# Scan products by 64-row halves in turn, and a rotation of score banks, in a two-network kernel on one core

## The chip, the core and the metric

The kernel runs on one core of a Trainium2 chip. The core has TensorE for matrix products (it writes into PSUM, eight banks of 128 partitions by 512 fp32 columns), VectorE, ScalarE and GpSimd for everything element by element, SyncE which mainly issues transfers, and 16 DMA engines. Each engine works through its own list of instructions in order; semaphores tie the lists together. The metric is device time of one execution in microseconds; less is better. [...]

## The reference, cut to what matters

Two small networks run one after the other on 256 tokens of width 1024. The first layer of the first network has two mixers side by side for 256 latent and 256 context tokens: a gated delta rule that is scanned in chunks of 64 tokens, in both directions, and a latent attention with eight heads. The scan of one direction, cut:

```
def step(s, inp):
    u_i, w_i, qk_i, qd_i, kd_i, gl_i = inp
    v_new = u_i - einsum('bhck,bhkv->bhcv', w_i, s)
    o_i = einsum('bhck,bhkv->bhcv', qd_i, s) + einsum('bhcs,bhsv->bhcv', qk_i, v_new)
    s = s * gl_i[..., None, None] + einsum('bhck,bhcv->bhkv', kd_i, v_new)
    return s, o_i
```

There are 8 heads, keys and values of 64, and 512 tokens (context first, then latent), so 8 steps in each direction, 16 in all. The attention, cut:

```
s = einsum('bqkgd,bskd->bkgqs', q_i, k).astype(float32) * scale
p = softmax(s, axis=-1)
return einsum('bkgqs,bskd->bqkgd', p, v)
```

Context tokens see 256 keys, latent tokens 512.

## The kernel before

All is in fp32. Large products split each operand into a high and a low part (`whi`, `wlo`) and are three products (`mm3`, L554 to L556); ScalarE casts the high part (L270), VectorE or GpSimd subtracts for the low part (L272). Weights come by SyncE's queue into a ring of raw buffers (`wraw`), two in this stretch. Small fp32 products are given to TensorE as they are; each of them is two instructions there.

A scheduler with its own model of time sets the order in which each engine's instructions stand; a tile (PSUM bank or buffer) is handed on in the order in which the program asks for tiles of its kind. In the first layer PSUM has kinds `g` (three banks, also what `aux` asks for), `s` (two, also `acc`), `tp`, `po` and `gv` (one each).

The scan is `gdn_run`. Its outer loop has four blocks of 128 tokens (two chunks, one in partitions 0 to 63, the other in 64 to 127); inside it come the two directions `d`. `gdn_operands` (L1142) makes, for a direction and block, `u` (L1158), `w` transposed (L1160) and the queries transposed (L1163) in three `g` banks, which ScalarE copies to `gu` and `gwq` (L1165 to L1169), and loads `Q` (the masked query-key products) by SyncE's queue (L1171). `gdn_state` then does one step: operands times state (L1192), the difference `gvn` on VectorE (L1195), the state products (L1199, four of 128 columns, of which the 64x64 blocks on the diagonal are used), the decay of the state on GpSimd (L1206), its sum on VectorE (L1207), and the query products (L1210, eight of 64 columns); `gdn_o` adds results to the output (L1177). `gdn_post` follows (L1238 to L1245).

After the scan in the program, and mixed with it by the scheduler, come six modulation products (`mod_chunk`: loads L370, products L373, columns L386) and `l0_mla`. It works by four pairs of heads; a pair's queries and keys are projected (L849 to L857), then four query tiles go through `attend`: scores, maximum (L676), exponential (L678), transposes into the same bank (L681), copy `pt` (L683), row sums (L699), value products (L689). Score banks are both `s` in pairs 0 and 1, one `s` and one `g` in pairs 2 and 3, whose projections use `g` as well. The buffers `p` and `pt` are two each (`K.np`).

Of the kernel before, what the change touches and what calls it, by code (L numbers as in the profile page):

```python
# [15 lines left out]
ALU = mybir.AluOpType  # L16
# [192 lines left out]
def aux(K):  # L209
    return bank(K, "aux")  # L210
# [576 lines left out]
def l0_mla(K, O):  # L787
# [44 lines left out]
    for t in range(4):  # L832
# [2 lines left out]
        mm3(K, ps, ch[:, tk], cl[:, tk], wkh[:, 1, :], wkl[:, 1, :], True, True)  # L835
        nc.scalar.copy(vt[:, t, :], ps)
    wq = None
    for pair in range(4):
        heads = {}
        for h in (2 * pair, 2 * pair + 1):  # L840
            if h % 4 == 0:
                wq = WQ.load(K.ins["w_q"], 0, 2, (h // 4) * 512, 512)
            late = "g" if pair >= 2 else None
            ps = bank(K, late or "acc")
            hs = slice((h % 4) * 128, (h % 4 + 1) * 128)
            for k in range(2):
                mm3(K, ps, wq[0][:, k, hs], wq[1][:, k, hs], qh[:, k, :], ql[:, k, :], k == 0, k == 1)
            u = cut(K, [128, 512], F32, "p", K.np)
            nc.vector.tensor_tensor(u, ps, K.c("qtab"), op=ALU.mult)  # L849
            q1, q2 = cut(K, [128, 512], FR, "q1", 2), cut(K, [128, 512], FR, "q2", 2)  # L850
            split(K, q1, q2, u)
            ps = bank(K, late or "acc")
            hs = slice(h * 64, (h + 1) * 64)
            mm3(K, ps[:64, :], wkh[:, 0, hs], wkl[:, 0, hs], ch, cl, True, True)
            k1, k2 = kh[h % 2], kl[h % 2]
            nc.scalar.copy(k1[:64, :], ps[:64, :])
            nc.vector.tensor_tensor(k2[:64, :], ps[:64, :], k1.bitcast(F32)[:64, :], op=ALU.subtract)  # L857
            heads[h] = (q1, q2, k1, k2)
        po, rb = bank(K, "po"), bank(K, "gv")
        for t in range(4):  # L860
            n = 256 if t < 2 else 512

            def score(pss):
                tk = slice(t * 128, (t + 1) * 128)
                for hh in range(2):
                    q1, q2, k1, k2 = heads[2 * pair + hh]
                    mm3(K, pss[hh][:, :n], q1[:, tk], q2[:, tk], k1[:, :n], k2[:, :n], True, True)
                    yield pss[hh][:, :n]
            attend(K, score, lambda hh, j: vt[:, j, pair * 128 + hh * 64:pair * 128 + hh * 64 + 64], po, rb, t * 128,
                   ("s", "g") if late else ("s", "s"))  # L870
        nc.scalar.copy(O[:, pair, :], rb)
        nc.vector.tensor_tensor(O[:, pair, :], po, O[:, pair, :], op=ALU.mult)

# [264 lines left out]
def gdn_operands(K, d, t):  # L1140

    nc = K.nc  # L1142
    q, k, v = K.qkv
    P = K.P[d]
    tv = lambda x: x[:, t, :].rearrange("p (h d) -> p h d", h=8)
    sc = lambda x: bc(x[:, t * 8:(t + 1) * 8], [128, 8, 64], 2)
    ke = cut(K, [128, 8, 64], F32, "gke", 1)
    qe = cut(K, [128, 512], F32, "gqe", 1).rearrange("p (h d) -> p h d", h=8)
    kd = cut(K, [128, 512], F32, "gkd", 2)
    nc.vector.tensor_tensor(ke, tv(k), sc(K.eg[d]), op=ALU.mult)  # L1150
    nc.vector.tensor_tensor(qe, tv(q), sc(K.eg[d]), op=ALU.mult)
    nc.gpsimd.tensor_tensor(kd.rearrange("p (h d) -> p h d", h=8), tv(k), sc(K.ekd[d]), op=ALU.mult)
    pu, pw = aux(K), [aux(K), aux(K)]
    for h in range(8):
        hs = slice(h * 64, h * 64 + 64)
        for a in range(2):
            r = slice(a * 64, a * 64 + 64)
            nc.tensor.matmul(pu[r, hs], P[r, t, h, :], v[r, t, hs], start=True, stop=True)  # L1158
            o = (h // 2) * 64
            nc.tensor.matmul(pw[a][(h % 2) * 64:(h % 2) * 64 + 64, o:o + 64], ke[r, h, :], P[r, t, h, :],  # L1160
                             start=True, stop=True)
    for p in range(4):
        nc.tensor.transpose(pw[p // 2][:, 256 + p % 2 * 128:384 + p % 2 * 128], qe[:, 2 * p:2 * p + 2, :].rearrange("p h d -> p (h d)"), K.ident)  # L1163
    u = cut(K, [128, 512], F32, "gu", 2)
    nc.scalar.copy(u, pu)  # L1165
    wq = cut(K, [128, 4, 4, 64], F32, "gwq", 2)
    for a in range(2):
        nc.scalar.copy(wq[:, :, 3 * a, :], pw[a][:, :256].rearrange("p (q c) -> p q c", q=4))
        nc.scalar.copy(wq[:, 2 * a:2 * a + 2, 1:3, :], pw[a][:, 256:].rearrange("p (q a c) -> p q a c", q=2, a=2))  # L1169
    Q = cut(K, [128, 8, 64], F32, "gQ", 2)  # L1170
    nc.sync.dma_start(Q, K.Qd[d, t].rearrange("p (h c) -> p h c", h=8))  # L1171
    return u, wq, kd, Q


def gdn_o(K, t, a, o, ps):
    if (t, a) in K.owritten:
        K.nc.vector.tensor_tensor(K.O[o, t, :], K.O[o, t, :], ps[o], op=ALU.add)  # L1177
    else:
        K.owritten.add((t, a))
        K.nc.scalar.copy(K.O[o, t, :], ps[o])  # L1180


def gdn_state(K, d, first, t, a, u, wq, kd, Q, S):
    nc = K.nc
    r = slice(64 * a, 64 * a + 64)
    o = slice(64 - 64 * a, 128 - 64 * a)
    if first:
        vn = u
    else:
        ps = aux(K)  # L1190
        for p in range(4):
            nc.tensor.matmul(ps[:, p * 128:(p + 1) * 128], wq[:, p, 2 * a:2 * a + 2, :].rearrange("p x c -> p (x c)"),  # L1192
                             S[:, p, :], start=True, stop=True)
        vn = cut(K, [128, 512], F32, "gvn", 2)
        nc.vector.tensor_tensor(vn[r], u[r], ps[r], op=ALU.subtract)  # L1195
    pS, po = aux(K), aux(K)
    for p in range(4):
        c = slice(p * 128, (p + 1) * 128)
        nc.tensor.matmul(pS[:, c], kd[r, c], vn[r, c], start=True, stop=True)  # L1199
    pSv = pS.rearrange("p (q c) -> p q c", q=4)  # L1200
    for hh in range(2):
        x = slice(hh * 64, hh * 64 + 64)
        if first:
            nc.vector.tensor_copy(S[x, :, x], pSv[x, :, x])
        else:
            nc.gpsimd.tensor_tensor(S[x, :, x], S[x, :, x], bc(K.glc[d][x, t, a, :], [64, 4, 64], 2), op=ALU.mult)  # L1206
            nc.vector.tensor_tensor(S[x, :, x], S[x, :, x], pSv[x, :, x], op=ALU.add)  # L1207
    for h in range(8):
        hs = slice(h * 64, h * 64 + 64)
        nc.tensor.matmul(po[o, hs], Q[r, h, :], vn[r, hs], start=True, stop=True)  # L1210
    if not first:
        gdn_o(K, t, a, o, ps)
    gdn_o(K, t, a, o, po)


def gdn_run(K):
    K.owritten = set()
    for i in range(4):
        for d in range(2):
            t = i if d == 0 else (1, 0, 3, 2)[i]  # L1220
            ops = gdn_operands(K, d, t)
            for a in ((0, 1) if d == 0 else (1, 0)):
                gdn_state(K, d, i == 0 and a == d, t, a, *ops, K.S[d])


def gdn_post(K):
# [951 lines left out]
```

## Time and profile before

| | |
|---|---|
| median of 3 runs | 2125.01 us (2121.82 to 2138.47) |
| the profiled execution | 2124.6 us |
| its span, first to last instruction | 2122.8 us |
| mean granted clock | 0.957 |
| TensorE busy | 1991.6 us, 94% |
| VectorE busy | 1315.5 us, 62% |
| ScalarE busy | 924.7 us, 44% |
| scan and latent attention | about 269 to 456 us of the span |

Busy time of an engine is the union of its instructions' durations. [...] Idle time is put down to what released the engine. A stretch in which an engine is busy all the time at a low clock is longer than its work.

### The profile page before, as it was taken

The numbers are of one execution on the slowest core, as the hardware profiler recorded it, in microseconds if no ns is written. First come the engines' busy times: TensorE is split into PE (matmuls) and PEld (weight loads), VectorE is DVE, ScalarE is ACT, GpSimd is POOL, SyncE is SP. The second block draws the span as 40 slices with busy tenths as digits, with TensorE's granted clock in tenths as the row PEclk, the third lists the DMA queues.
The fourth block names the chain that finished last, engine by engine and source line by source line (L and its number), as shares of the span: only waits on it lengthen the run. The fifth ranks groups of instructions, "written<-read, shape, count | busy, mean of one in ns | idle before, by whom it ended". The sixth has DMA issues, their size and how long they took to land.

```text
span 2122.8 us, 31144 instructions
## 1 busy us (share of the span) xinstructions
PE 1991.6 (94%) x11656; PEld 1626.7 (77%) x11656; DVE 1315.5 (62%) x2729; ACT 924.7 (44%) x1620; POOL 242.1 (11%) x312
## 2 busy tenths in 40 slices
PE   6989799889999999979898999998999999989998
PEld 3868468768888778868666888897788789868886
DVE  5557457766777754454786555575765558576644
ACT  4533443354222233343565443564554445555532
POOL 2120212301000000020401001110200021020000
PEclk8999789899999999989898999998999999999999
DMA  8344542132568542213235664522656535055551
GB/s 284 90 120 101 179 130 66 46 109 80 179 213 279 164 158 90 89 53 120 70 99 159 184 194 137 155 87 62 197 179 190 180 97 147 21 169 184 188 188 66
DMA packets 186951, 291.88 MB, mean 137 GB/s; under 512 B 28472, under 2 KB 75704, under 8 KB 186800
## 3 DMA queue, kind: packets, MB, share of 16 engines
q1 hardware_dynamic: 172720, 272.54, 41.2%
q0 software_dynamic: 5472, 16.13, 2.4%
q10 hardware_dynamic: 8608, 1.23, 0.5%
q8 instruction: 91, 1.49, 0.3%
q14 instruction: 60, 0.49, 0.1%
HBM read 281.44 MB, written 8.41 MB: 137 GB/s over the span
## 4 chain that ended last, share of the span: by engine, by line
PE 85%; DVE 5%; DMA 4%; ACT 3%; issue 2%; POOL 1%; SPq 0%; ACTq 0%; DVEq 0%; POOLq 0%
PE acc L554 19%; PE acc L556 19%; PE acc L555 19%; PE s L554 3%; PE s L555 2%; PE s L556 2%; PE po L689 2%; PE tp L890 2%; PE po L1540 1%; PE tp L1540 1%; DMA wraw<-in_w_mod_dram 1%; PE gv L373 1%; PE aux L728 1%; PE aux L489 1%; PE g L1199 1%
## 5 line engine op out<-in xcount | busy, mean ns | idle before, releaser
L272 DVE TENSOR_TENSOR wlo<-wraw,whi 128x512 fp32r<-128x512 f32 (+4 forms) x772 | 483.4, 670 | 299.1 <-ACT whi L270 283.3
L270 ACT CAST whi<-wraw 128x1024 fp32r<-128x1024 f32 (+4 forms) x420 | 413.5, 990 | 496.4 <-PE acc L556 192.9
L554 PE MATMUL acc<-whi,u 128*128 128x512 f32 (+3 forms) x1320 | 508.5, 388 | 15.4 <-ACT u L306 9.6
L556 PE MATMUL acc<-whi,u 128*128 128x512 f32 (+3 forms) x1320 | 505.2, 384 | 1.7 <-DVE u L307 1.7
L555 PE MATMUL acc<-wlo,u 128*128 128x512 f32 (+3 forms) x1320 | 506.0, 385 | 0.2 <-DVE wlo L272 0.2
L554 PEld LDWEIGHTS acc<-whi,u 128*128 128x128 f32 x1320 | 251.3, 191 | 66.0 <-ACT u L306 11.6
L556 PEld LDWEIGHTS acc<-whi,u 128*128 128x128 f32 x1320 | 251.0, 190 | 50.4 <-DVE u L307 3.8
L555 PEld LDWEIGHTS acc<-wlo,u 128*128 128x128 f32 x1320 | 251.4, 191 | 47.4 <-DVE wlo L272 1.4
L554 PE MATMUL acc<-u,whi 128*128 128x512 f32 (+1 forms) x480 | 171.0, 362 | 1.8 <-ACT u L306 1.7
L555 PE MATMUL acc<-u,whi 128*128 128x512 f32 (+1 forms) x480 | 171.0, 358 | 0.2 <-DVE u L307 0.2
L556 PE MATMUL acc<-u,wlo 128*128 128x512 f32 (+1 forms) x480 | 171.1, 360 | 0.0
L272 POOL TENSOR_TENSOR wlo<-wraw,whi 128x512 fp32r<-128x512 f32 (+1 forms) x68 | 84.7, 1276 | 409.7 <-ACT whi L270 409.7
L432 DVE SCALAR_TENSOR_TENSOR msum<-mraw,u,msum 128x512 f32<-128x512 f32 x140 | 100.8, 747 | 15.2 <-DMA mraw<-in_w_mod_dram 14.1
L554 PEld LDWEIGHTS acc<-u,whi 128*128 128x128 f32 x480 | 91.0, 191 | 17.4 <-issue 2.6
L555 PEld LDWEIGHTS acc<-u,whi 128*128 128x128 f32 x480 | 91.9, 192 | 15.0 <-issue 1.7
L556 PEld LDWEIGHTS acc<-u,wlo 128*128 128x128 f32 x480 | 91.5, 191 | 15.0 <-issue 1.7
L307 DVE TENSOR_TENSOR u<-aux,u 128x512 fp32r<-128x512 f32 (+2 forms) x96 | 59.5, 632 | 41.0 <-ACT u L306 40.8
L554 PE MATMUL acc<-whi,dxh 128*128 128x512 f32 x176 | 69.7, 396 | 1.9 <-ACT dxh L306 1.9
L306 ACT CAST u<-aux 128x512 fp32r<-128x512 f32 (+2 forms) x96 | 50.6, 543 | 47.6 <-PE aux L728 34.9
L555 PE MATMUL acc<-wlo,dxh 128*128 128x512 f32 x176 | 69.6, 396 | 0.0
L556 PE MATMUL acc<-whi,dxl 128*128 128x512 f32 x176 | 69.0, 396 | 0.0
L307 DVE TENSOR_TENSOR dxl<-u,dxh 128x1024 fp32r<-128x1024 f32 x22 | 26.7, 1225 | 52.5 <-ACT dxh L306 52.5
(521 smaller groups left out, 3089.6 us busy)
## 6 DMA issues: line engine op xcount, KB each, us to landing
wraw<-in_w_up_dram SPq DMA_DIRECT2D x64, 512.0 KB, 4.0
wraw<-in_w_down_dram SPq DMA_DIRECT2D x64, 512.0 KB, 4.0
mraw<-in_w_mod_dram SPq DMA_DIRECT2D x56, 512.0 KB, 4.7
wraw<-in_w_ffn_down_dram SPq DMA_DIRECT2D x44, 512.0 KB, 3.8
wraw<-in_w_mod_dram SPq DMA_DIRECT2D x40, 512.0 KB, 5.9
wraw<-in_w_ffn_gate_dram SPq DMA_DIRECT2D x48, 256.0 KB, 3.1
wraw<-in_w_ffn_up_dram SPq DMA_DIRECT2D x48, 256.0 KB, 3.6
wraw<-in_w_ffn_gate_dram SPq DMA_DIRECT2D x20, 512.0 KB, 4.5
```

Source lines behind the costliest of these rows:

```text
L270: self.K.nc.scalar.copy(hi, raw)
L272: e.tensor_tensor(lo[:, k], raw[:, k], hi.bitcast(F32)[:, k], op=ALU.subtract)
L306: (hi_eng or nc.scalar.copy)(hi, src)
L307: nc.vector.tensor_tensor(lo, src, hi.bitcast(F32), op=ALU.subtract)
L373: nc.tensor.matmul(ps[32 * j:32 * j + 32, :], K.cl[:, g + k, :], raw[:, k, :], start=(g + k < 4), stop=(g + k >= 4))
L432: nc.vector.scalar_tensor_tensor(accs[s], raw[:, k, :], c, accs[s], op0=ALU.mult, op1=ALU.add)
L554: mm(ps, ah, bh, start=start, stop=False)
L555: mm(ps, ah, bl, start=False, stop=False)
L556: mm(ps, al, bh, start=False, stop=stop)
L689: nc.tensor.matmul(po[hh * 64:hh * 64 + 64, c:c + 128], v(hh, j), pts[hh][0][:, j * 128:(j + 1) * 128], start=(j == 0), stop=(j == nj - 1))
L890: nc.tensor.matmul(tp[:, t * 128:(t + 1) * 128], x[:, t // 2, t % 2 * 128 + j:t % 2 * 128 + j + 128], dg[j], start=(j == 0), stop=(j == 4))
L1540: nc.tensor.matmul(ps[t][:, c * 128:c * 128 + 128], yp[:, c, t * 128 + j:t * 128 + j + 128] if j < 31 else ones, dg, start=(j == 0), stop= ...
```

## The change

In the scan the two directions of a block are taken together: operands of both first, then for each of the two halves a step of either direction, which stand in opposite halves of the partitions. The state products become eight of 64x64 and 64 columns instead of four of 128 columns: only the diagonal blocks, by the column halves in turn. The query products of the two directions go into one bank, a head of one direction and the same head of the other in turn, so that the row and the column half switch at each product. The addition of the product with the state (`gdn_o` of `ps`) stands before the state products in the program.

In the latent attention `p` and `pt` get three buffers, and the score banks rotate: `s`, `s`, `tp` in pairs 0 and 1, `s`, `s`, `tp`, `g`, `g`, `g` in pairs 2 and 3.

```diff
@@ l0_mla
+    used = [0]
+    def unit(kinds):
+        used[0] += 2
+        return [kinds[(used[0] + i) % len(kinds)] for i in range(2)]
+    K.np = 3
     for pair in range(4):
...
             attend(K, score, lambda hh, j: vt[:, j, pair * 128 + hh * 64:pair * 128 + hh * 64 + 64], po, rb, t * 128,
-                   ("s", "g") if late else ("s", "s"))
+                   unit(("s", "s", "tp", "g", "g", "g") if late else ("s", "s", "tp")))
...
+    K.np = 2
@@ gdn_state
-def gdn_state(K, d, first, t, a, u, wq, kd, Q, S):
+def gdn_state(K, d, first, t, a, u, wq, kd, S):
...
         nc.vector.tensor_tensor(vn[r], u[r], ps[r], op=ALU.subtract)
-    pS, po = aux(K), aux(K)
+        gdn_o(K, t, a, slice(64 - 64 * a, 128 - 64 * a), ps)
+    pS = aux(K)[:, :256].rearrange("p (q c) -> p q c", q=4)
     for p in range(4):
-        c = slice(p * 128, (p + 1) * 128)
-        nc.tensor.matmul(pS[:, c], kd[r, c], vn[r, c], start=True, stop=True)
-    pSv = pS.rearrange("p (q c) -> p q c", q=4)
+        for hh in range(2):
+            c = slice(p * 128 + hh * 64, p * 128 + hh * 64 + 64)
+            nc.tensor.matmul(pS[hh * 64:hh * 64 + 64, p, :], kd[r, c], vn[r, c], start=True, stop=True)
...
-            nc.vector.tensor_tensor(S[x, :, x], S[x, :, x], pSv[x, :, x], op=ALU.add)
-    for h in range(8):
-        hs = slice(h * 64, h * 64 + 64)
-        nc.tensor.matmul(po[o, hs], Q[r, h, :], vn[r, hs], start=True, stop=True)
-    if not first:
-        gdn_o(K, t, a, o, ps)
-    gdn_o(K, t, a, o, po)
+            nc.vector.tensor_tensor(S[x, :, x], S[x, :, x], pS[x], op=ALU.add)
+    return vn
@@ gdn_run
-        for d in range(2):
-            t = i if d == 0 else (1, 0, 3, 2)[i]
-            ops = gdn_operands(K, d, t)
-            for a in ((0, 1) if d == 0 else (1, 0)):
-                gdn_state(K, d, i == 0 and a == d, t, a, *ops, K.S[d])
+        ts = [i, (1, 0, 3, 2)[i]]
+        ops = [gdn_operands(K, d, ts[d]) for d in range(2)]
+        for s in range(2):
+            vns = []
+            for d in range(2):
+                u, wq, kd, Q = ops[d]
+                a = s ^ d
+                vns.append((64 * a, Q, gdn_state(K, d, i == 0 and s == 0, ts[d], a, u, wq, kd, K.S[d])))
+            po = aux(K)
+            for h in range(8):
+                hs = slice(h * 64, h * 64 + 64)
+                for a, Q, vn in vns:
+                    K.nc.tensor.matmul(po[64 - a:128 - a, hs], Q[a:a + 64, h, :], vn[a:a + 64, hs], start=True, stop=True)
+            for d in range(2):
+                a = s ^ d
+                gdn_o(K, ts[d], a, slice(64 - 64 * a, 128 - 64 * a), po)
```

The scheduler draws new orders for all engines from this. Three places follow; a row is the line in that kernel's own file, the operation, the tile written and those read. In the changed kernel L1166, L1168 and L1171 are the operand products, L1200 operands times state, L1209 the state products, L1237 the query products, L1173 the copy of `gu`.

On TensorE, the end of the scan before, from the last direction's last transposes on (`g_3964` is a projection of pair 2):

```order
L1163 MATMUL g_3051<-const_id_75,gqe_3044 128x128 x2
L1192 MATMUL g_3097<-u_130,gwq_3090 128x128 x4
L1199 MATMUL g_3104<-gvn_3102,gkd_3045 128x128 x4
L1210 MATMUL g_3105<-gvn_3102,gQ_3095 64x64 x8
L1192 MATMUL g_3124<-u_130,gwq_3090 128x128 x4
L1199 MATMUL g_3131<-gvn_3129,gkd_3045 128x128 x4
L1210 MATMUL g_3132<-gvn_3129,gQ_3095 64x64 x8
L554 MATMUL g_3964<-u_3380,whiq_3958 128x512
```

The same place in the changed kernel, the last half of the last block (`s_` and `tp_` are scores of pair 1, `u_129` and `u_130` the states of the two directions):

```order
L1200 MATMUL g_3146<-u_129,gwq_3024 128x128 x4
L556 MATMUL tp_3869<-u_3441,q_3856 128x256
L681 MATMUL s_3868<-const_id_75,p_3875 128x128 x2
L1209 MATMUL g_3154<-gvn_3151,gkd_2979 64x64 x8
L1200 MATMUL g_3167<-u_130,gwq_3078 128x128 x4
L689 MATMUL po_3865<-pt_3879,u_3444 64x128
L554 MATMUL s_3901<-u_3441,q_3855 128x256
L555 MATMUL s_3901<-u_3443,q_3855 128x256
L556 MATMUL s_3901<-u_3441,q_3856 128x256
L681 MATMUL tp_3869<-const_id_75,p_3886 128x128 x2
L681 MATMUL s_3900<-const_id_75,p_3907 128x128 x2
L699 MATMUL gv_3866<-const_id_75,rs_3892 128x128
```

The attention of pair 1, which before stands ahead of the last steps, now stands between them; after the second state products come the sixteen query products of both directions.

On ScalarE of the changed kernel, the operands of the third block (`g_2753` to `g_2755` the first direction's banks, `g_2807` and `g_2808` the second's; `wraw_4482` is a part of w_out_even):

```order
L1173 COPY gu_2792<-g_2753 128x512
L1176 COPY gwq_2794<-g_2754 128x4x64
L1177 COPY gwq_2794<-g_2754 128x2x128
L375 COPY mrow_3426<-gv_3409 128x512
L683 COPY pt_3725<-s_3714 128x256
L1176 COPY gwq_2794<-g_2755 128x4x64
L1177 COPY gwq_2794<-g_2755 128x2x128
L270 CAST whi_4483<-wraw_4482 128x1024
L1173 COPY gu_2846<-g_2807 128x512
L1176 COPY gwq_2848<-g_2808 128x4x64
```

The weight cast stands ahead of the copy that frees `g_2807`; before, the cast of the same kind stood between an exponential of the attention and the next, behind both copies of its block.

On ScalarE in the second layer, where the second network's sine tables are made beside the attention, the order before:

```order
L678 ACTIVATE p_9075,sm_9058<-tp_9059,nmx_9073 128x512
L683 COPY pt_9004<-acc_8973 128x512
L678 ACTIVATE p_9085,sm_9058<-tp_9060,nmx_9083 128x512
L1472 ACT_TABLE_LOAD
L1472 ACTIVATE u_10983<-u_10997 128x2x8
L1475 ACTIVATE u_10982<-u_10985 128x2x8
L678 ACT_TABLE_LOAD
```

and in the changed kernel:

```order
L678 ACTIVATE p_9131,sm_9114<-tp_9115,nmx_9129 128x512
L1489 ACT_TABLE_LOAD
L1489 ACTIVATE u_11039<-u_11053 128x2x8
L683 COPY pt_9060<-acc_9029 128x512
L678 ACT_TABLE_LOAD
L678 ACTIVATE p_9141,sm_9114<-tp_9116,nmx_9139 128x512
L1492 ACT_TABLE_LOAD
L1492 ACTIVATE u_11038<-u_11041 128x2x8
L678 ACT_TABLE_LOAD
```

An exponential stands between the two, so four table loads stand where there were two: 15 in the program in place of 13.

## Rows read from the trace of the kernel before

**Rows 1.** The page, part 1: busy time, share and instructions of each engine.
```profile
PE 1991.6 (94%) x11656; PEld 1626.7 (77%) x11656; DVE 1315.5 (62%) x2729; ACT 924.7 (44%) x1620; POOL 242.1 (11%) x312
```
**Rows 2.** Stretches: length, busy us of each engine, granted clock, DMA share, GB/s.
```profile
269.00:284.00 15.00, 13.95 (x128) 10.89 (x128) 7.82 (x24) 5.69 (x12) 1.22 (x2) 0.66 0.27 93
284.00:356.00 72.00, 70.39 (x745) 53.89 (x743) 46.38 (x82) 30.08 (x65) 12.15 (x17) 1.00 0.36 111
356.00:366.00 10.00, 8.64 (x103) 7.91 (x103) 6.35 (x12) 3.77 (x11) 2.31 (x3) 0.66 0.10 28
366.00:396.00 30.00, 29.47 (x353) 24.51 (x352) 20.14 (x34) 9.12 (x24) 5.91 (x9) 1.00 0.04 11
396.00:413.00 17.00, 13.90 (x74) 11.95 (x75) 10.70 (x26) 3.71 (x9) 7.01 (x11) 0.62 0.28 87
413.00:456.00 43.00, 38.52 (x243) 27.48 (x241) 31.18 (x60) 21.07 (x55) 8.53 (x12) 0.95 0.20 64
...
269.00:456.00 187.00, 174.87 (x1639) 136.61 (x1638) 122.58 (x236) 73.44 (x174) 37.13 (x52) 0.91 0.24 76
```
**Rows 3.** Order of time, TensorE, 330 to 344 us: start, length, line, product.
```profile
330.12 1.16 PE L1199 MATMUL g<-gvn,gkd 64*128 64x128 f32 x8
331.20 1.14 PE L1210 MATMUL g<-gvn,gQ 64*64 64x64 f32 x16
332.27 0.71 PE L699 MATMUL gv<-const_id,rs 128*128 128x128 f32 x4
...
334.75 1.06 PE L1192 MATMUL g<-u,gwq 128*128 128x128 f32 x8
...
339.43 0.98 PE L1158 MATMUL g<-u,u 64*64 64x64 f32 x27
340.34 0.49 PE L699 MATMUL gv<-const_id,rs 128*128 128x128 f32 x2
340.76 1.09 PE L689 MATMUL po<-pt,u 128*64 128x128 f32 x14
341.77 0.50 PE L554 MATMUL s<-u,q 128*128 128x512 f32 x1
...
343.10 0.85 PE L1160 MATMUL g<-u,gke 64*64 64x64 f32 x32
343.89 0.66 PE L1163 MATMUL g<-const_id,gqe 128*128 128x128 f32 x4
```
**Rows 4.** Groups by line, TensorE, 262 to 462 us: the query products.
```profile
L1210 PE MATMUL g<-gvn,gQ 64*64 64x64 f32 x224 | 18.4, 241 | 0.0
...
L1210 PE MATMUL g<-gu,gQ 64*64 64x64 f32 x32 | 3.1, 268 | 0.0
```
**Rows 5.** Order of time, TensorE, the end of the scan.
```profile
399.69 1.79 PE L1199 MATMUL g<-gvn,gkd 64*128 64x128 f32 x8 [1.18 <-DVE gvn L1195]
401.41 1.96 PE L1210 MATMUL g<-gvn,gQ 64*64 64x64 f32 x16
```
**Rows 6.** Waits of TensorE, 269 to 456 us: total, times, longest.
```profile
PE s L681 <- ACT p L678: 3.0, 5, 1.8
...
PE g L554 <- ACT q L306: 1.7, 1, 1.7
```
**Rows 7.** Order of time: SyncE issues w_out_even, ScalarE casts it.
```profile
325.74 0.89 SPq L276 DMA_DIRECT2D wraw<-in_w_out_even_dram  x2
...
330.82 1.04 ACT L270 CAST whi<-wraw 128x1024 fp32r<-128x1024 f32 x1 [2.67 <-DMA wraw<-in_w_out_even_dram]
```
**Rows 8.** Order of time: SyncE issues w_mod, TensorE waits for it.
```profile
304.25 14.53 SPq L370 DMA_DIRECT2D wraw<-in_w_mod_dram  x6
...
309.33 1.05 PE L373 MATMUL gv<-wraw,u 128*32 128x512 f32 x4 [1.10 <-DMA wraw<-in_w_mod_dram]
```
**Rows 9.** The chain that ended last, at the sine tables.
```profile
1042.29 1.28 ACT L1472
1043.92 1.28 ACT L678
```

## The prediction before the result

> **What bounds the kernel now.** I read the page first: TensorE is busy for 94% of the span and VectorE for 62% [rows 1], so most of the time is TensorE's, but the change touches one stretch only. That stretch I found by the lines of the scan (L1192, L1199, L1210): they run from 269 to 411 us, mixed with modulation products and with the first two head pairs of the latent attention; the other two pairs follow to 456 us. So I cut the table of stretches there [rows 2]. [...] VectorE is busy for 122.6 of the whole 187 us, ScalarE for 73.4 [rows 2]: no bound on average, though each runs its list in order.
>
> The view in order of time gives the pace of each kind of product, as the distance to the next row's start [rows 3]. The four state products (eight instructions, since an fp32 product is two) take 331.20 - 330.12 = 1.08 us, 135 ns each; the eight query products take 332.27 - 331.20 = 1.07 us, 67 ns each. The operand products, also 64x64 but with the row halves in turn, go at 0.79/32 = 25 ns (L1160) and 0.91/27 = 34 ns (L1158). The attention's value products, full rows with the column halves in turn, go at 1.01/14 = 72 ns for 128 columns.
>
> **The change, part by part.** All durations are of the profiled execution, which took 2124.6 us, 0.4 us under the median.
>
> Query products. There are 16 steps (two directions, four blocks, two halves); the counts, 224 + 32 query instructions at sixteen a step, confirm it [rows 4]. Before: 16 x 1.07 = 17.1 us. Now two steps share 32 instructions that switch both row half and column half at each product. The nearest rows are the operand products, 25 to 34 ns [rows 3]; at 28 ns a pair costs 0.90 us, eight pairs 7.2. Gain 9.9 us; bounds 17.1 - 8 x 32 x 0.025 = 10.7 at best and, if nothing overlaps (67 ns), 0.
>
> [...] The operand products of L1158 write both halves of one bank from two row halves, and go at 34 ns, not 67 [rows 3]. [...]
>
> State products. Before: 1.08 us a step, 17.3 in all. Now sixteen instructions a step, 64 columns each, on the same 64 rows, the column half alone in turn. The trace has no such row. Best: the 25 ns of L1160, 0.40 us, a gain of 0.68 x 16 = 10.9 us. Worst: the 72 ns of the value products, which also switch columns alone, 1.15 us, a loss of 1.1 us in all. 67 ns, L1210's pace in one corner, is no change. I take 55 ns, nearer to L1210 since the rows do not alternate: 0.88 us, a gain of 0.20 x 16 = 3.2 us.
>
> The end of the scan. From 396 to 413 us TensorE is busy for 13.9 of 17 us at clock 0.62 [rows 2]. It waits twice over 1 us for VectorE's difference (L1195), and in between its products run at half pace: 1.72 us from the start of the state products to that of the query products, and 1.96 for these [rows 5]. The order before has nothing between the last steps; now transposes, scores and sums of pair 1 stand between them, and pair 2 begins without a gap. Two steps at full pace need 2 x (1.06 + 1.08 + 1.07) = 6.4 us (1.06 for the product of state and operands, L1192 [rows 3]), and the 2.6 us of projections that follow at half pace 1.3 at full, so 17 - 7.7 = 9.3 us are to be had. Where only one score product and two transposes stand before the state products (some 0.35 us) the 0.69 us difference still shows, so I take 6.5; bounds 0 and 9.3.
>
> Attention banks. In the last 43 us TensorE idles 4.5 [rows 2]; over the whole stretch it waits 3.0 us for exponentials before transposes and once 1.7 us for a query cast [rows 6]. Three buffers and a third kind of bank let a score start before the last one's copies are done. The exponential's and the copy's own time on ScalarE and VectorE stays. I take 2 us; bounds -1 and 4.5.
>
> What is moved, and what it is moved past. Operands of both directions now come first. Three "g" banks serve both sets, so the first product with the state (L1192, now L1200) of a block waits for the second direction's copy gu. In the third block ScalarE's order has a weight cast of w_out_even ahead of that copy. Before, that load was issued at 325.7 us, when the last modulation product freed its buffer, and the cast began at 330.8, after 2.7 us of waiting [rows 7]: 5.1 us. Now TensorE has some 5 us of work between these two points (at the paces of rows 3: the rest of the first direction's operands 0.4 + 0.3, the second's 0.9 + 0.8 + 0.7, and some 1.6 for transposes, modulation columns and a row sum, an estimate at 110 to 190 ns each), while the cast and the copy end 5.1 + 1.05 + 0.59 = 6.7 us after: a wait of 2 us. VectorE has the two low parts (1.3 us) behind the same cast; the difference queued after them is covered by 2 us of scores and value products. Cost 2 us; bounds 0 and 4.
>
> SyncE's queue: the two loads of Q for a block are issued together, behind one more pair of w_mod loads than before; that pair no longer stands behind a Q load which waits for a query product. But in the first two blocks the pair of w_mod products is followed by less work (transposes 0.9, state 0.9, operands times state 1.1 = 2.9 us) than the 309.33 - 304.25 = 5.1 us from a load's issue to its product [rows 8]. Two waits of 2 us, less the 1.1 us waited today and some 0.4 for the pair that is issued earlier: cost 2.5 us; bounds 0 and 5.
>
> ScalarE's tables: in layer 1 the scheduler now puts one exponential between sine and cosine, so two more table loads of 1.28 us [rows 9]. Both loads of today lie on the chain that ended last, so I take 2 of the 2.6 us; bounds 0 and 2.6. Everything else in the program differs by neighbours swapped, at no cost: the same products, between the same loads.
>
> Sum: 9.9 + 3.2 + 6.5 + 2 - 2 - 2.5 - 2 = 15.1 us. 2124.6 - 15.1 = **2109.5 us**.
>
> **Rivals.**
> (a) The column halves overlap as the row halves do. For it: L1158 and L1160 are at 25 to 34 ns though part of their neighbours share rows; against it, 72 ns for the value products [rows 3]. The state then gains 9 us in place of 3, and with the end of the scan at its 9.3 the sum is 15.1 + 5.8 + 2.8 = 23.7: about 2101 us, down to 2096 if the load waits also vanish. [...] Chance 0.24.
> (b) The products do not pair up: one bank, or the weight loads, keep them near 67 ns. For it only that the query's weights differ at each product; against it L1158. Both first terms go, and the rest is 2 us: 2122 us. Chance 0.08.
> (c) The clock. Each low stretch began beside a run of 64-row products with a gap after it [rows 2, 5]. Now a block has the query products and both directions' operands in one run, 0.9 + 2 x 2.0 and transposes, some 6 us against 3.3. If blocks two and three each bring one stretch like 356 to 366, 10 us at 0.66 or 3.4 us lost, 7 us go: 2116 us. Against it: the 3.3 us runs between 284 and 356 us leave the clock at 1.00. Chance 0.20.
> (d) Slower. The bank wait of the third block comes in all three later blocks, since the second direction's copies share ScalarE with the exponentials, and each brings a stretch like 396 to 413 [rows 2]: 17 us at 0.62 lose 6.5, idle 3.1, the wait itself 2, together 11.6 a block and 35 us in all, against gains of 15.1 + 2 = 17.1 without that wait: 2124.6 + 35 - 17 = 2142. It outweighs the gains from 5.7 us a block on. Against it: the weight cast stands in one block only, and the products with the state have other work behind them. Chance 0.05.
>
> **How the numbers follow.** The forecast has 0.43, with its own range of 2104 to 2115. The range that leaves out 2 in 10 runs from 2097 (most of a) to 2121 (c, and half of b). One per cent, 21 us, is about what a measurement of this kernel can tell from no change; the runs lie 2121.8 to 2138.5. Faster by over 1% means under 2103.8: most of (a), 0.20, and 0.08 of the forecast's lower end, 0.28. Slower by over 1%: (d), 0.04. Within: 0.68.
>
> **What would show it.** Query products at 25 to 34 ns an instruction in runs of 32 (a wrong first term: 67). State products: 16 instructions in 0.88 us. No stretch of clock under 0.9 at the scan's end, and TensorE's last scan product some 12 us earlier. A wait of L1200 for gu once, in the third block, of 2 us; 15 table loads on ScalarE in place of 13. I am wrong if a new half-clock stretch follows each operand run, or if VectorE's or ScalarE's order holds TensorE for over 2 us in several blocks.

## The result, and the profile after

The changed kernel takes 2101.08 us (median of four runs, 2098.82 to 2103.51) against 2123.88 us of before, a ratio of 0.9878 with the interval 0.9832 to 0.9925. Run again later, beside the last experiments, it took 2099.01 us (six runs, 2092.0 to 2102.79) against 2126.64, ratio 0.9866, 0.9842 to 0.9891. So it is some 1.2 to 1.3% faster by the ratios, and 23 and 28 us lie between the medians, where 15.1 us were forecast. The profiled execution took 2103.28 us, with a span of 2101.5 us, 21.3 us less than before's 2122.8.

The page after, part 1, answers to [rows 1]: 23.4 us less of TensorE's busy time and 19.6 less of its weight loads (PEld), 4.2 less of VectorE's, the rest within 2 us.

```profile
PE 1968.2 (94%) x11784; PEld 1607.1 (76%) x11784; DVE 1311.3 (62%) x2729; ACT 926.7 (44%) x1622; POOL 241.5 (11%) x312
```

The table of stretches after, with the columns of [rows 2]:

```profile
269.00:284.00 15.00, 13.13 (x274) 11.05 (x269) 10.62 (x31) 9.36 (x20) 1.49 (x3) 1.00 0.37 109
284.00:356.00 72.00, 67.64 (x955) 50.77 (x954) 50.59 (x90) 29.61 (x68) 18.14 (x24) 1.00 0.36 116
356.00:366.00 10.00, 7.25 (x87) 5.65 (x87) 7.33 (x12) 4.95 (x10) 2.79 (x4) 0.99 0.01 2
366.00:376.00 10.00, 9.86 (x89) 8.67 (x90) 9.33 (x24) 1.98 (x7) 2.50 (x5) 0.50 0.00 0
376.00:396.00 20.00, 19.70 (x167) 14.73 (x166) 17.02 (x37) 8.63 (x20) 7.77 (x12) 1.00 0.34 107
396.00:426.00 30.00, 27.65 (x216) 21.07 (x215) 24.84 (x47) 18.48 (x50) 4.98 (x6) 1.00 0.21 71
```

Before, TensorE was busy for 70.39 of the 72 us from 284 us and for 29.47 of the 30 from 366 us, both at the clock of 1.00 [rows 2]; work taken off it there could be time gained, unless a wait took its place. The granted clock is given as a share of the full one. In windows of 1 us it is 1.00 or 0.50 from 269 us to the end of the stretch, before and after, but for the windows in which it changes; half clock stands for 0.50. The query products of before start an instruction every 58 or 59 ns at 1.00 and every 106 or 107 ns at 0.50 (from 401.4 us on). The three half-clock stretches of before, in the rows from 269, 356 and 396 us (0.66, 0.66 and 0.62 [rows 2]), are gone in this profile; one is new, 366 to 376 us at 0.50, behind 2.75 idle us in the ten before it. The stretch ends 29.4 us sooner: the transposes that open the output projection (L1269, before L1252) start at 426.1 us, not 455.5, and the last query product at 379.3, not 410.1.

TensorE in order of time, with the columns of [rows 3]: one step, then the end of a second and the query products of the pair.

```profile
303.89 0.68 PE L1209 MATMUL g<-gvn,gkd 64*64 64x64 f32 x16
304.50 1.16 PE L1200 MATMUL g<-u,gwq 128*128 128x128 f32 x8
...
309.58 0.51 PE L1209 MATMUL g<-gvn,gkd 64*64 64x64 f32 x10
309.88 0.27 PE L1237 MATMUL g<-gvn,gQ 64*64 64x64 f32 x1
309.92 0.28 PE L1209 MATMUL g<-gvn,gkd 64*64 64x64 f32 x3
309.98 0.22 PE L1237 MATMUL g<-gvn,gQ 64*64 64x64 f32 x1
309.99 0.27 PE L1209 MATMUL g<-gvn,gkd 64*64 64x64 f32 x2
310.04 0.22 PE L1237 MATMUL g<-gvn,gQ 64*64 64x64 f32 x1
310.05 0.22 PE L1209 MATMUL g<-gvn,gkd 64*64 64x64 f32 x1
310.10 1.09 PE L1237 MATMUL g<-gvn,gQ 64*64 64x64 f32 x29
311.12 1.16 PE L1200 MATMUL g<-u,gwq 128*128 128x128 f32 x8
```

The state products of a step take 304.50 - 303.89 = 0.61 us, 38 ns an instruction, against 1.08 us [rows 3]. The sixteen of state and 32 of query from 309.58 to 311.12 take 1.54 us, which leaves 0.93 us for the query products, 29 ns each, against 67.

These means hold the start and the end of a run. The recorded starts of single instructions tell more; an instruction of 64x64 lasts 218 ns in the trace, longer than the distance to the next start. Call the half of the partitions that a product's operands stand in (row half), together with the half that its result goes to (column half), a quarter. At the clock of 1.00 products of one quarter alone start an instruction every 58 ns (the query products of before, median of 168 distances). Two quarters in turn keep 58 ns each here, whether they differ in the column half alone (state, 303.89 us) or in both halves (query): the rows of L1237 above at 309.98, 310.04 and 310.10 are one quarter's. So two quarters start an instruction every 29 ns, 0.46 us for sixteen, and the step's 0.61 us hold some 0.15 us more at the two ends of the run, where another shape follows.

TensorE's longest waits after, 262 to 430 us, answer to [rows 6]:

```profile
PE gv L373 <- DMA wraw<-in_w_mod_dram: 2.4, 2, 1.4
PE tp L555 <- DVE u L864: 2.1, 1, 2.1
PE g L1200 <- ACT gu L1173: 1.4, 1, 1.4
PE s L681 <- ACT p L678: 1.0, 2, 0.6
```

Not all of the lead of 29.4 us arrives. At the second network's first value products it is 26.7 us (1429.9 against 1456.6 us), at the first activation of its up-projection 21.6 (1488.5 against 1510.1), at the end 21.3. Most of the loss lies in that second piece. In the table of stretches it is this row before:

```profile
1456.60:1510.10 53.50, 48.01 (x217) 38.13 (x216) 36.82 (x83) 26.12 (x51) 12.04 (x10) 0.86 0.53 167
```

and this row after:

```profile
1429.90:1488.50 58.60, 52.64 (x217) 42.18 (x217) 36.90 (x83) 25.99 (x50) 12.59 (x10) 0.79 0.49 153
```

The same 217 products are busy 4.6 us longer at a lower clock.

### The profile page after: what moved, and what is told of

Read it like the earlier page. It is cut to its first block, busy times and chain, and to the rows that moved or that the text cites. A ratio compares the mean times of both kernels' runs of the same rounds, so it can differ in the third digit from the quotient of the medians.

```text
span 2101.5 us, 31402 instructions
## 1 busy us (share of the span) xinstructions
PE 1968.2 (94%) x11784; PEld 1607.1 (76%) x11784; DVE 1311.3 (62%) x2729; ACT 926.7 (44%) x1622; POOL 241.5 (11%) x312
## 4 chain that ended last, share of the span: by engine, by line
PE 82%; DVE 7%; DMA 5%; ACT 3%; issue 2%; POOL 0%; ACTq 0%; SPq 0%; DVEq 0%; POOLq 0%
PE acc L554 19%; PE acc L556 18%; PE acc L555 18%; PE s L554 3%; PE s L555 2%; PE s L556 2%; PE po L689 2%; PE tp L898 2%; PE po L1557 1%; PE tp L1557 1%; DMA wraw<-in_w_mod_dram 1%; DVE wlo L272 1%; PE gv L373 1%; DMA mraw<-in_w_mod_dram 1%; PE aux L489 1%
## 5 line engine op out<-in xcount | busy, mean ns | idle before, releaser
L554 PE MATMUL acc<-whi,u 128*128 128x512 f32 (+3 forms) x1320 | 509.7, 389 | 13.4 <-ACT u L306 7.5
L554 PEld LDWEIGHTS acc<-u,whi 128*128 128x128 f32 x480 | 90.2, 190 | 17.9 <-issue 2.6
L555 PEld LDWEIGHTS acc<-u,whi 128*128 128x128 f32 x480 | 90.8, 189 | 15.1 <-issue 1.7
L307 DVE TENSOR_TENSOR dxl<-u,dxh 128x1024 fp32r<-128x1024 f32 x22 | 26.7, 1225 | 54.3 <-ACT dxh L306 54.3
```

Source lines behind the costliest of these rows:

```text
L307: nc.vector.tensor_tensor(lo, src, hi.bitcast(F32), op=ALU.subtract)
L554: mm(ps, ah, bh, start=start, stop=False)
L555: mm(ps, ah, bl, start=False, stop=False)
```

## Experiments

A whole run scatters by 4 to 25 us from execution to execution, so small prices are read from the profiles. For each kernel one row of the table of stretches was taken, from the first operand product to the first transpose of the output projection. Busy time x granted clock is work at full speed, busy time x (1 - clock) is what the half clock cost, the rest is idle (us; the clock has two digits, so the first two carry some 0.8 us). The first two are estimates: they take the pace as proportional to the clock, and the query products of before take 1.8 times as long at 0.50, not twice (107 against 58 ns). Each row is one execution. The work is no exact count of products: banks alone has the products of before and scan alone those of the changed kernel, yet their work differs by 4.0 and 5.3 us.

| kernel | stretch | busy | clock | work | half clock | idle | whole, ratio to before (95%) |
|---|---|---|---|---|---|---|---|
| before | 186.5 | 174.37 | 0.91 | 158.7 | 15.7 | 12.1 | 1 |
| changed | 156.9 | 145.12 | 0.97 | 140.8 | 4.4 | 11.8 | 0.9878 (0.9832, 0.9925) |
| changed, again | 155.7 | 145.18 | 0.97 | 140.8 | 4.4 | 10.5 | 0.9866 (0.9842, 0.9891) |
| old order, state halves | 179.7 | 165.75 | 0.92 | 152.5 | 13.3 | 13.9 | 0.9962 (0.9942, 0.9982) |
| new order, both old forms | 171.8 | 164.87 | 0.93 | 153.3 | 11.5 | 6.9 | 0.9959 (0.9935, 0.9984) |
| state of 128 columns | 160.5 | 151.52 | 0.98 | 148.5 | 3.0 | 9.0 | 0.9884 (0.9852, 0.9916) |
| query one direction after the other | 157.3 | 147.52 | 0.98 | 144.6 | 3.0 | 9.8 | 0.9887 (0.9858, 0.9916) |
| state half by half | 155.3 | 145.77 | 0.99 | 144.3 | 1.5 | 9.5 | 0.9891 (0.9839, 0.9942) |
| query in two banks | 164.4 | 150.34 | 0.94 | 141.3 | 9.0 | 14.1 | 0.9890 (0.9835, 0.9945) |
| state of both in turn | 154.2 | 142.10 | 0.98 | 139.3 | 2.8 | 12.1 | 0.9870 (0.9841, 0.9900) |
| banks alone | 183.0 | 168.12 | 0.92 | 154.7 | 13.4 | 14.9 | 0.9986 (0.9957, 1.0015) |
| scan alone | 169.3 | 150.62 | 0.97 | 146.1 | 4.5 | 18.7 | 0.9881 (0.9846, 0.9916) |
| low part on GpSimd | 152.5 | 141.36 | 1.00 | 141.4 | 0.0 | 11.1 | 0.9853 (0.9831, 0.9875) |
| one sine | 155.5 | 143.51 | 0.98 | 140.6 | 2.9 | 12.0 | 0.9848 (0.9824, 0.9873) |

**State halves in the old order.**

```diff
 # before.py, gdn_state
...
-        nc.tensor.matmul(pS[:, c], kd[r, c], vn[r, c], start=True, stop=True)
+        for hh in range(2):
+            c = slice(p * 128 + hh * 64, p * 128 + hh * 64 + 64)
+            nc.tensor.matmul(pS[hh * 64:hh * 64 + 64, p, :], kd[r, c], vn[r, c], start=True, stop=True)
...
```

> The kernel before with the state products alone changed to eight of 64 columns that switch column halves; order of steps, query products and banks as before. If the switch of column halves is worth the same in the old order: 0.61 us a step against 1.08, full-clock work 7.5 us less, the output projection's first transposes at 448 us against 455.5, and about 2116 us in all, with the half-clock loss of before (19 us) still there. Rival (shorter steps spare the half clock too): 10 us or more less of it, transposes at 438 us or earlier, about 2107 us.

TensorE in order of time:

```profile
308.72 0.68 PE L1201 MATMUL g<-gvn,gkd 64*64 64x64 f32 x16
309.24 1.09 PE L1211 MATMUL g<-gvn,gQ 64*64 64x64 f32 x16
```

0.52 us a step here, where products of the same shape follow, and 0.9962: 8.1 us off the whole, between 4 and 12, about what the shorter steps are worth. In the profile 13.3 us are still lost to the half clock; that execution is the longest of its ten (2112.08 to 2123.29). The first theory held; shorter steps alone did not spare the half clock there.

**State of 128 columns in the new kernel.**

```diff
 # after.py, gdn_state
...
-        for hh in range(2):
-            c = slice(p * 128 + hh * 64, p * 128 + hh * 64 + 64)
-            nc.tensor.matmul(pS[hh * 64:hh * 64 + 64, p, :], kd[r, c], vn[r, c], start=True, stop=True)
+        nc.tensor.matmul(pS[:, c], kd[r, c], vn[r, c], start=True, stop=True)
...
```

> The changed kernel with the state products of a step as four of 128 columns again, instead of eight of 64 that switch column halves. If the halves carry what the trace of after shows (0.61 us a step against 1.08): 16 steps of 0.47 us, 7.5 us later at the output projection's first transposes (433.6 us against 426.1) and about 2109 us in all. If the state steps lie behind waits, under 3 us of this shows.

TensorE in order of time, a step's state products and the query products behind them:

```profile
309.66 1.16 PE L1208 MATMUL g<-gvn,gkd 64*128 64x128 f32 x8
310.75 1.15 PE L1237 MATMUL g<-gvn,gQ 64*64 64x64 f32 x32
311.83 0.94 PE L1200 MATMUL g<-u,gwq 128*128 128x128 f32 x6
```

A step takes 1.09 us again, and the work of the stretch grows by 7.7 us, as expected. But the stretch grows by 3.6 only, since idle time and half clock shrink by 4.2: part of the dearer work seems to fill time in which TensorE would wait, which one profile does not prove. Neither theory as a whole. The row also gives the query products by themselves, with nothing beside them: 1.08 us for 32, 34 ns.

**State half by half.**

```diff
 # after.py, gdn_state
-    for p in range(4):
-        for hh in range(2):
+    for hh in range(2):
+        for p in range(4):
```

> The changed kernel with the state products of a step in another order: the four of the left column half first, then the four of the right one, so that the column half switches once instead of at each product. If the switch from product to product is what makes them quick: 67 ns an instruction as the query products of before, 1.07 us a step. If it is only that 64 columns are streamed in place of 128 and the blocks off the diagonal are left out: 0.61 us a step as in the changed kernel.

TensorE in order of time, a step with nothing of the scan ahead of it:

```profile
298.84 0.96 PE L1209 MATMUL g<-gvn,gkd 64*64 64x64 f32 x16
299.74 1.16 PE L1200 MATMUL g<-u,gwq 128*128 128x128 f32 x8
```

0.90 us, 56 ns an instruction. The same products at the same size: with the column half switched at each product 38 ns, switched once 56. The smaller size alone gives next to nothing: sixteen 64-column instructions in one quarter take 1.07 us, the query products of [rows 3], against 1.08 for eight of 128 columns. Of the 0.47 us saved in a step the one switch gives 0.17, since by the recorded starts the two halves overlap where they meet, and the other switches give 0.29. So the first theory held, but for that overlap. The two runs, 2100.12 and 2103.85 us, tell no price of the whole.

**State of both directions in turn.**

```diff
 # after.py: first both differences gvn, then, with a bank for each direction
...
+            for p in range(4):
+                for hh in range(2):
+                    c = slice(p * 128 + hh * 64, p * 128 + hh * 64 + 64)
+                    for d in range(2):
+                        r = slice(64 * (s ^ d), 64 * (s ^ d) + 64)
+                        nc.tensor.matmul(pS[d][hh * 64:hh * 64 + 64, p, :], ops[d][2][r, c], vns[d][r, c], start=True, stop=True)
...
```

> The changed kernel with the state products of both directions of a pair in turn too, each direction in its own bank, so that the row half switches as well as the column half. If rows and columns in turn give the pace of the operand products (25 to 29 ns against 38): up to 2.3 us less full-clock work. If the wait for the second direction's difference (0.69 us of VectorE) holds all 32 products: 0.7 us of new wait in each of up to seven pairs, 2 us or more slower.

TensorE in order of time, a pair of steps whose state products stand in turn:

```profile
331.71 0.73 PE L1226 MATMUL g<-gvn,gkd 64*64 64x64 f32 x27
332.23 0.22 PE L1241 MATMUL g<-gvn,gQ 64*64 64x64 f32 x1
...
332.35 1.15 PE L1241 MATMUL g<-gvn,gQ 64*64 64x64 f32 x30
333.43 0.38 PE L386 MATMUL gv<-const_id,mrow 128*128 128x2 f32 x2
```

Where both directions' state products do stand in turn, 64 instructions take 1.72 us, 27 ns each, against 2 x 0.61 + 0.93 = 2.15 in the changed kernel. The 32 of state, which use all four quarters in turn, start within 0.64 us, 20 ns each. But the scheduler parted the directions in several of the eight pairs (at 304.86 us sixteen of one stand alone). 1.5 us less work, 1.6 more idle than the changed kernel run beside it, 2098.79 against 2099.01 us: no gain to be measured.

**Query products one direction after the other.**

```diff
 # after.py, gdn_run
-            for h in range(8):
-                hs = slice(h * 64, h * 64 + 64)
-                for a, Q, vn in vns:
+            for a, Q, vn in vns:
+                for h in range(8):
+                    hs = slice(h * 64, h * 64 + 64)
```

> The changed kernel with the query products of a pair of steps one direction after the other, so that neither the row half nor the column half switches from product to product; the bank is the same. If the switch of halves is what makes them quick: 32 instructions take about 2.1 us (67 ns each) in place of 0.93, eight pairs lose 9.6 us, the output projection's first transposes come at 436 us and the whole takes about 2111 us. If it is the grouping of 32 products in one run that makes them quick: pace and time stay as in the changed kernel.

TensorE in order of time, the same place as in the changed kernel at 309.58 us:

```profile
307.63 0.51 PE L1209 MATMUL g<-gvn,gkd 64*64 64x64 f32 x10
307.92 0.27 PE L1237 MATMUL g<-gvn,gQ 64*64 64x64 f32 x1
...
308.15 1.67 PE L1237 MATMUL g<-gvn,gQ 64*64 64x64 f32 x29
309.75 0.49 PE L1200 MATMUL g<-u,gwq 128*128 128x128 f32 x2
```

The run of 48 takes 2.12 us against 1.54, so eight pairs lose 4.6 us of work (3.8 by the table), half of what was expected. The first direction's products stand in the row half that the state products ahead of them leave free, and start before those have all started (307.92 us); by the recorded starts the two directions overlap in the same way where they meet, and between these places an instruction starts every 58 ns. The stretch is 0.4 us longer, no more; idle time and half clock give back the rest. So the switch is what makes them quick, but both theories missed the size.

**Query products in two banks.**

```diff
 # after.py, gdn_run
-            po = aux(K)
+            pos = aux(K), aux(K)
...
```

> The changed kernel with the query products of the two directions in two PSUM banks, still in turn. [...] If the bank does not matter: 0.93 us as before, and the extra bank costs only waits.

TensorE in order of time, a step and the query products of its pair, and the products of one direction at another place:

```profile
288.75 0.51 PE L1209 MATMUL g<-gvn,gkd 64*64 64x64 f32 x10
...
289.27 1.10 PE L1237 MATMUL g<-gvn,gQ 64*64 64x64 f32 x29
290.30 0.70 PE L373 MATMUL gv<-wraw,u 128*32 128x512 f32 x4
...
315.18 1.14 PE L1237 MATMUL g<-gvn,gQ 64*64 64x64 f32 x16
316.25 0.44 PE L689 MATMUL po<-pt,u 128*64 128x128 f32 x4
```

The bank does not matter for the pace. In two of the eight pairs the directions stand in turn, and the 48 instructions take 1.55 us here (288.75 to 290.30) and 1.54 at 358.00 us, against 1.54 with one bank. In the others the scheduler, free of the common bank, put most or all of the two directions apart; sixteen of one by themselves take 1.07 us, the 67 ns of before.

**The order with both old forms.** The two diffs together, of the 128 columns and of one direction after the other.

> The changed kernel's order of steps and its banks, with both kinds of product in their old forms: state products of 128 columns, query products one direction after the other. If the order spares the half clock by itself: of the stretch from 262 us to the output projection's first transposes, the part lost to the half clock stays near 5 to 7 us (18.9 before, 7.3 in the changed kernel), full-clock work is 145.0 + 7.7 + 4.1 = 157 us, those transposes come at about 433 us and the whole takes about 2108 us. Rival (the quick products are what spares the half clock, since they shorten the runs of 64-row products): 15 us or more at the half clock again, transposes at 443 us or later, 2118 us or more.

TensorE in order of time, again a step's state products and a pair's query products:

```profile
311.29 1.16 PE L1208 MATMUL g<-gvn,gkd 64*128 64x128 f32 x8
312.37 1.90 PE L1237 MATMUL g<-gvn,gQ 64*64 64x64 f32 x32
314.20 1.05 PE L1200 MATMUL g<-u,gwq 128*128 128x128 f32 x7
```

The transposes come at 441.1 us, near the rival: 11.5 us are lost to the half clock, nearly all in one piece from 373 to 397 us. This execution is among the longer of its ten (2120.89 us; 2106.09 to 2126.93). The order and the banks give 8.7 us of the whole (3 to 14), and in this profile little of the clock. With either form alone undone the loss is 3.0 us, again in one profile each. That does not make one quick form enough: with two query banks, where the state keeps its quick form, 9.0 us are lost.

**Banks alone, scan alone.**

```diff
 # banks alone: gdn_state and gdn_run of before; scan alone, l0_mla:
-    K.np = 3
...
-                   unit(("s", "s", "tp", "g", "g", "g") if late else ("s", "s", "tp")))
+                   ("s", "g") if late else ("s", "s"))
...
-    K.np = 2
```

> The attention's part of the change alone: three buffers and the bank rotation, with the scan as it was before. As predicted (the banks are worth 2 us): state steps at 1.08 us and query steps at 1.07 us as in [rows 3], the first transposes of the output projection some 2 us earlier than the 455.5 us of before, about 2122 us in all. Rival (the banks are what fills the scan's waits and spares it the half clock): those transposes 10 us or more earlier, at 445 us, and about 2114 us in all.

> The scan's part alone: array halves and the new order of the steps, with the attention's banks and two buffers as before. As predicted (nearly all comes from the scan): the transposes of the output projection within 3 us of the 426.1 us of the changed kernel, about 2103 us in all. Rival (the banks carry 10 us or more of the lead): these transposes at 436 us or later, 2111 us or more in all.

The banks alone give 0.9986, 3 us less with an interval of 9 less to 3 more. The scan alone is at 0.9881, like the whole change, which speaks against the rival of 10 us from the banks. But its profiled execution, the longest of its four (2110.76 us, the others 2099.01 to 2104.3), has a stretch 12.4 us longer than the changed kernel's, 7 to 8 us of it idle time. The medians give the banks 1 to 4 us; the intervals do not shut out 10.

**The changed kernel again, and the low part of w_q on GpSimd.**

```diff
 # after.py, l0_mla
     WK, WQ = Weights(K, K.cur, 1, 1, "k"), Weights(K, K.cur, 1, 1, "q")
+    WQ.turn("V", "P")
```

> The changed kernel itself, once more, beside the next three on one chip. If the half clock behind the gap at 362 to 366 us belongs to the program, a second profile shows it again, 4 to 5 us, and the scan up to the output projection's first transposes takes 157 us within 2 us. If such stretches wander from run to run, it lies elsewhere or has another length, and the median lies anywhere from 2098 to 2104 us.

> The changed kernel with the low part of the second half of w_q (wloq, 1.70 us of VectorE at 361.21 us) made by GpSimd, so that VectorE reaches the key's low part, for which TensorE waits 2.1 us at 364 us, sooner. If that gap is what the half clock from 366 to 375 us follows: both go, 2 us of idle time and 4.9 us of half clock, the stretch from the first operand products to the output projection's first transposes takes about 150 us in place of 157. If the half clock comes beside 64-row products whatever the gap: the idle time shrinks by 2 us and the 4 to 5 us at half clock stay.

VectorE in the changed kernel, first profile, at the place:

```profile
361.21 1.70 DVE L272 TENSOR_TENSOR wloq<-wraw,whiq 128x512 fp32r<-128x512 f32 x2
362.83 0.86 DVE L1216 TENSOR_TENSOR u<-u,g 64x256 f32<-64x256 f32 x2
363.72 0.68 DVE L864 TENSOR_TENSOR u<-s,u 64x512 fp32r<-64x512 f32 x1
```

TensorE waits 2.1 us for the last of them. Stretches of the changed kernel run again:

```profile
361.00:362.00 1.00, 0.74 (x4) 0.53 (x4) 0.97 (x3) 0.00 (x0) 0.00 (x0) 0.98 0.00 0
362.00:369.00 7.00, 6.22 (x75) 5.73 (x75) 6.42 (x16) 0.94 (x3) 1.22 (x2) 0.51 0.00 0
```

and of the one with the low part on GpSimd:

```profile
356.00:361.00 5.00, 5.00 (x72) 3.89 (x71) 2.23 (x4) 4.01 (x9) 1.74 (x3) 1.00 0.00 0
361.00:366.00 5.00, 3.87 (x65) 3.24 (x64) 4.88 (x11) 1.08 (x2) 3.17 (x4) 1.00 0.01 5
366.00:376.00 10.00, 8.75 (x106) 6.55 (x107) 9.64 (x21) 2.78 (x10) 3.61 (x7) 1.00 0.21 74
```

Run again, the changed kernel has the same wait of 2.1 us and the half clock behind it, so it belongs to the program; its stretch is 155.7 us. (It has a short piece at half clock besides, 273.2 to 276.6 us, where the first profile is at 1.00.) With the low part on GpSimd the wait is 0.46 us, the clock stays at 1.00 throughout, and the stretch takes 152.5 us: the first theory, though other waits grew and kept the idle time at 11.1. Of the whole, 2096.12 against 2099.01 us; the intervals overlap, so no gain is claimed. The other profiles of the new order agree: each has a wait of 1.6 to 2.6 us in this part, between 358 and 375 us, and the half clock begins there no later than 1.5 us after its end. How long it then lasts, 3 to 24 us, the wait does not tell, and a wait of 1.56 us at 344 us with two query banks is followed by none.

**One sine.**

```diff
 # after.py, rope2_tables
...
-            nc.scalar.activation(K.rs[:, :, 8:16], r, AF.Sin)
...
-            nc.scalar.activation(K.rc[:, :, 0:8], r, AF.Sin)
...
+    nc.scalar.activation(both, both, AF.Sin)
...
```

> The changed kernel with sine and cosine of layer 1 in one activation, so that ScalarE loads 13 tables in place of 15. If the two loads lie on the path as predicted: 2 us less in layer 1, of the whole too. If other work hides them: less than 0.5 us from the first rest of the projection's columns (the copy lx) to the second network's first convolution, beside what the clock does there.

From the first copy `lx` of the last columns to the first convolution it takes 393.0 us (959.0 to 1352.0), the changed kernel 394.7 and 396.5, so 1.7 and 3.5 us less. But the kernel with state of 128 columns also loads 13 tables, by its order, and takes 396.0, and the one with the low part on GpSimd loads 15 and takes 392.1. So this piece moves by more than the loads are worth, and does not show their price. 2096.3 against 2099.01 us for the whole, intervals overlapping: not settled.

## Why the prediction came out as it did

It forecast 2109.5 us, 2097 to 2121, and 2101 came, the time of rival (a), which had 0.24. The direction and most terms held; two were too small, and one loss was not in the sum. That the time meets (a)'s is partly luck: up to the output projection the lead is 29.4 us, where (a)'s terms make 25.7, and 8.1 are lost behind, where (a) has the 2 of the tables. It is faster by over 1%, which had 0.28.

- **Query products, +9.9.** 29 ns an instruction in place of the assumed 28: 17.1 - 8 x 0.93 = 9.7 us. Two row halves in one bank, where they write different halves of its partitions, did not hinder each other here: 1.54 us with one bank, 1.54 and 1.55 with two. So rival (b) did not come.
- **State products, +3.2.** This step failed. "I take 55 ns, nearer to L1210 since the rows do not alternate" was the wrong neighbour: it is 38 ns, 16 x 0.47 = 7.5 us. Half by half they go at 56, so what counts is that the column half switches at each product, and that was what rival (a) said. [rows 3] spoke for it already. The 72 ns of the value products, taken as the worst case and as evidence against (a), are for 128 columns. The state products of before, 128 columns without a switch, took 135, so with the column half in turn 128 columns went at about half. In the step at 303.89 us, all in one row half, the weight loads run beside the products: the sixteen loads take 0.54 us in all, and the third starts at 303.95 us, between the second product's start (303.90) and the third's (304.00):

```profile
303.89 0.54 PEld L1209 LDWEIGHTS g<-gvn,gkd 64*64 64x64 f32 x16 [0.36 <-issue]
```

- **The end of the scan, +6.5.** The half clock at 396 us is gone, but so are those at 269 and 356 us, which the sum had left alone. In the whole stretch the half clock falls from 15.7 to 4.4 us, 11.3, and idle time stays (12.1, 11.8). With the 17.2 of the two products that is 28.8 of the 29.4 us of lead; the forecast had 17.1 by then. By the table the work falls by 17.9, but the kernel with both old forms in the new order has 5.4 less already, some 2.5 of it because its two directions of query products overlap where they meet (1.83 us a pair, not 2.14). Why the clock stays up was not found: ahead of the three low stretches of before stand waits of 1.0, 1.75 and 1.2 us, but the changed kernel, in its first profile, has waits of 0.9 to 1.4 us that none follows.
- **Banks, +2.** Some 1 to 4 us by the medians, not settled closer.
- **Waits.** For the copy `gu` 1.4 us once, in the third block (forecast 2); for w_mod 2.4 us in two waits, 1.3 more than before (forecast 2.5). Not foreseen: the 2.1 us for the key's low part behind the low part of w_q on VectorE, and the half clock that follows, 3 to 5 us.
- **Table loads, -2.** 15 as foreseen; the price is not shown: over that piece, kernels with 15 loads took 392.1 to 399.7 us, kernels with 13 took 392.4 to 396.0.
- **"Everything else ... at no cost".** This failed too: 8.1 of the 29.4 us are lost behind the stretch, 5.1 of them where the second network starts, at the clock of 0.79 against 0.86. All kernels with the new order take longer there than the 53.5 us of before (56.6 to 58.8), also the changed kernel run again (0.79). But it is not tied to that order: state halves in the old order takes 56.4 us there, at 0.81, and behind the stretch it takes 1676.7 us and banks alone 1673.7, like the changed kernel's 1675.4, against 1667.3 in the one profile of before. So that profile may be the odd one. The cause is open; no experiment went there.
- **Rival (c)** came once in the first profile, and smaller than feared: one stretch, behind a wait, not behind each operand run. **Rival (d)** did not come.

## What to carry to other kernels

Give small products to the quarters in turn, so that neighbours differ in row half, column half or both: for the 64x64 products of this kernel, at the clock of 1.00, one quarter alone made 67 ns an instruction, two in turn 29 to 38, four 20 to 25. When a row is taken as a neighbour, compare the same number of columns. Count what an edit takes off as work, half clock and idle time apart: in the profiles here either quick form could be undone for less than half of its work, and both together cost some 17 us of the whole (0.9959 against 0.9878). And look at the wait ahead of each stretch at the low clock: here, moving one subtraction cut the wait from 2.1 to 0.46 us, and the stretch at 0.50 behind it went (1.00 throughout).

## Not expected of the hardware

The query products start before all state products ahead of them on TensorE's list have started: at 309.88 us the first of them, from 309.92 us on six more of the state, the last at 310.05. TensorE was taken to work through its list in order like every engine; by the recorded starts it does not here, where the state products stand in one row half and this query product in the other.
